# Loading a head's tiles half a head ahead, parking three outputs in DRAM, and moving softmax arithmetic from VectorE to ScalarE and GpSimd, in the attention stage of a hybrid transformer layer

## The chip, the cores and the metric

The kernel runs on one core of a Trainium2 chip. The core has a matrix engine (TensorE, PE in the profile, with its weight loads counted apart as PEld), VectorE (DVE), ScalarE (ACT), GpSimd (POOL) and SyncE (SP, which here only issues DMAs). Each engine works through its own queue in order, and semaphores tie the queues together. The metric is the device time of one launch in microseconds (us); less is better.

## The reference

One encoder layer on 1024 tokens of width 1024, in float32: a half-step SwiGLU feed-forward, a mixer, a second feed-forward, a final RMSNorm. The change is in the mixer, between its input projection and its output projections:

```python
# A: 8 heads of 64, each 64-token chunk sees itself and 8 chunks before it
p = softmax(q k^T / 8 + bias_A);            y_a = p v
# B: 4 heads, two score maps each, values of width 128, chunk-causal
p = softmax over keys of (q k^T / 8 + bias_B), for r = 0, 1
y_b = rms_norm((p[0] - lam * p[1]) v, subln_g) * (1 - lambda_init)
x = x + (sigmoid(g_A) * (y_a W_A) + sigmoid(g_B) * (y_b W_B)) W_o
```

## The kernel before

The work is in stages one after the other: feed-forward 1, mixer projection, attention, the two branch projections and W_o, feed-forward 2. Attention is the block that opens the PSUM pool `ps2` (line 750). The projection has left q, k, a second copy of k (low-order part) and v in DRAM; attention reads them per "head" of the loop, of which there are eight: four pairs of A heads (`jobs_a(pr)`) and four B heads (`jobs_b(hb, filler)`).

A job is a Python generator; each `yield` ends one of its steps. An A job (block pair `sb_`, head `h`) does scores, softmax and scaling for two blocks of 128 queries (lines 840 to 849), passes a step, transposes the probabilities (853 to 855), passes on, and multiplies by v (857 to 877). A B job (query block `i`, with `(i + 1) * 128` keys) does two scores and two softmaxes (914 to 920), two reciprocals (922, 924), the factor r2 = -lam * rs0 / rs1 (925) and the sum pr[0] += r2 * pr[1] (927) in one VectorE instruction; then, a step later, transposes (933), then the product with v (940 to 944), the scaling by r1 and the norm (945 to 955), and last a small matmul `try` that transposes and scales the output into y (957 to 960).

`run` (811) interleaves the jobs: it starts one job per round and moves up to four older ones a step on, the newest first. This gives the program order. A list scheduler then puts every engine's queue in order by a simulated timeline, with program order as priority: an instruction goes into the queue when its inputs, and a free buffer for what it writes, are there in that simulation.

Buffers that matter: `big` (line 70) has 14 slots of 8 KB per partition. A head holds four of them (qs, ks, kl, vt, loaded by `load_qkv`, 757), one for its bias rows nb (A: one per pair; B: one per two heads; `bias_rows`, 798, eight DMAs and some memsets on GpSimd), and one for its output y. All eight outputs stay in slots until the branch projections. The loads of a head are issued by its own first job (823 to 829, 901 to 909), so they are queued behind the jobs before, as far as priority goes, and need free slots.

`branch_a` (881) is the filler: the product of the A outputs with W_A, 16 pieces of 12 matmuls (lines 128 to 130 through `mm3`), handed out at half a piece per B job (934 to 937). It needs only the A outputs. The product with W_B follows when attention is done (975 on). `split` (94) writes a value as a rounded high part and a rest: ScalarE rounds (97 or 99), VectorE or GpSimd subtracts (102 or 104). `rsqrt` (137) is a GpSimd `pow` on a column of 128 values.

Of the kernel before, what the change touches and what calls it, by code (L numbers as in the profile page):

```python
# [9 lines left out]
F32 = mybir.dt.float32  # L10
F32R = mybir.dt.float32r
AF = mybir.ActivationFunctionType
ALU = mybir.AluOpType
# [41 lines left out]
def hybrid_layer_kernel(ctx, tc, x, ffn1_norm, ffn1_w_in, ffn1_w_out, mix_norm, w_mix_in,  # L55
# [35 lines left out]
    nc.vector.memset(neg_half, -0.5)  # L91

# [426 lines left out]
    def drams(n, shape, name, dtype=F32):  # L519
        return [dram.tile(shape, dtype, name=f"{name}{i}") for i in range(n)]  # L520
# [53 lines left out]
    ta_d = drams(KT, [P, S], "ta")  # L574
    diag_a = dram.tile([A_HEADS, SKEW, EA], F32, name="diag_a")
# [173 lines left out]
    ys = []  # L749
    with tc.tile_pool(name="ps2", bufs=1, space=PSUM) as ps:  # L750
# [60 lines left out]
        def run(jobs, filler=None):  # L811
            live = []
            for step, job in enumerate(list(jobs) + [None] * 4):
                for g in [job] + live[::-1] if job else live[::-1]:
                    next(g, None)
                live = (live + [job] if job else live)[-4:]


        def jobs_a(pr):
            ctx_ = {}  # L820

            def job(sb_, h):
                if not ctx_:
                    ctx_["qkv"] = load_qkv(pr)
                    ctx_["y"] = big([P, 2, S], "y")
                    ys.append(ctx_["y"])
                    ctx_["nb"] = big([P, 2, S], "nb", F32)
                    for hh in range(2):
                        bias_rows(ctx_["nb"][:, hh, :WA], diag_a, 2 * pr + hh, EA, WA)
# [9 lines left out]
                pms = []  # L839
                for s, i in enumerate((i0, i1)):  # L840
# [6 lines left out]
                    nc.vector.reciprocal(out=ri, in_=rs)  # L847
# [30 lines left out]
            return [job(sb_, h) for sb_ in range(4) for h in range(2)]  # L878
# [18 lines left out]
        def jobs_b(hb, filler):  # L897
            ctx_ = {}

            def job(i):  # L900
                if not ctx_:
                    ctx_["qkv"] = load_qkv(4 + hb)
                    ctx_["y"] = big([P, 2, S], "y")
                    ys.append(ctx_["y"])
                    if hb % 2 == 0:
                        nbs.append(big([P, 2, S], "nb", F32))
                        for hh in range(2):
                            bias_rows(nbs[-1][:, hh, :], diag_b, hb + hh, EB, WB)
                    ctx_["nb"] = nbs[-1][:, hb % 2, :]
# [3 lines left out]
                pr, rs = [], []  # L913
                for r in range(2):
                    sc, n = scores(qkv, r, i, 0, w)
                    pm = raw_tile([P, WB], "pm")[:, :w]
                    s_ = small.tile([P, 1], F32, tag="rs", name="rs")
                    softmax(sc, n, nb[:, WB - w:], pm, s_)
                    pr.append(pm)
                    rs.append(s_)  # L920
                r1, r2 = (small.tile([P, 1], F32, tag="ri", name="ri") for _ in range(2))
                nc.vector.reciprocal(out=r1, in_=rs[0])

                nc.vector.reciprocal(out=r2, in_=rs[1])  # L924
                nc.vector.scalar_tensor_tensor(out=r2, in0=r2, scalar=neg_lam, in1=rs[0],
                                               op0=ALU.mult, op1=ALU.mult)
                nc.vector.scalar_tensor_tensor(out=pr[0], in0=pr[1], scalar=r2, in1=pr[0],
                                               op0=ALU.mult, op1=ALU.add)
# [27 lines left out]
                yield  # L956
                tr = ps.tile([P, 4, P], F32, tag="pt", bufs=2, name="try")
# [3 lines left out]
            return [job(i) for i in range(NT)]  # L961

        jobs, nbs = [], []
        for pr in range(4):
            jobs += jobs_a(pr)
        filler = branch_a()
        due = [0]
        for hb in range(4):
            jobs += jobs_b(hb, filler)
        run(jobs)  # L970
        for _ in filler:
            pass

# [82 lines left out]
```

## Time and profile before

| quantity | us |
| --- | --- |
| three timed runs | 2149.18, 2153.07, 2155.61 |
| median | 2153.07 |
| profiled execution | 2152.95 |
| its span in the trace | 2151.1 |
| PE / DVE / ACT / POOL busy over the span | 2080.7 / 1442.3 / 980.2 / 181.4 |
| attention, from the first score matmul to the last write of y | 1075.8 to 1352.6 |
| of it, B heads' first softmax at | 1182.04, 1208.73, 1253.23, 1294.49 |

The profiled execution lies within 0.2 us of the median of the timed runs. A view of the trace by stretches of time gives, for each engine, the busy us in that stretch (how many instructions in brackets), the clock granted to TensorE as a share of full speed, the mean share of time in which the 16 DMA engines were busy, and GB/s. Views of groups give a line of the kernel, an engine, an operation, out<-in by the program's names, how many, the busy us and the mean ns of one, and the idle time in front of it with what ended it. A timeline row is start, duration, engine, line, operation. TensorE's busy time is modelled from pipelined matmuls and overstates its work; the weight loads (PEld) follow it more closely, since each matmul has one.

### The profile page before, as it was taken

Reading aid. Unit: us, or ns where it says so; the run is one execution under the profiler, and the core shown is the slowest. Engines: PE = TensorE matmul, PEld = TensorE weight load, DVE = VectorE, ACT = ScalarE, POOL = GpSimd, SP = SyncE. Lnnn points to the kernel's source line nnn. Section 1 sums busy time; section 2 is a strip of 40 time slices with the busy share of each in tenths; the row PEclk is TensorE's granted clock in tenths of the full one; section 3 lists DMA queues with packets and bytes.
Section 4 is the critical chain, followed back from the end, with each engine's and each line's share of the span. In section 5 each row is a group of like instructions: output and inputs, shape, how many; then the busy total and the mean of one; then the engine's idle time right before and its main releaser. Section 6 shows DMA issues by size and latency. Waiting matters only on the chain.

```text
span 2151.1 us, 29100 instructions
## 1 busy us (share of the span) xinstructions
PE 2080.7 (97%) x10073; PEld 1738.7 (81%) x10073; DVE 1442.3 (67%) x2650; ACT 980.2 (46%) x1919; POOL 181.4 (8%) x282
## 2 busy tenths in 40 slices
PE   6999999999999999999999988999999999999997
PEld 5788888888888788899788877788788888888886
DVE  7666566677577756566488977558766656658566
ACT  5433333334446544444498665146433333334444
POOL 2120000000001000000066233001000000000001
PEclk9999999999999999999999999999999999999999
DMA  6653333294445544553683364634543333366334
GB/s 194 173 169 111 95 96 120 93 327 143 117 128 162 168 142 164 198 196 136 230 275 105 136 211 133 233 119 151 172 156 95 111 96 95 114 237 228 98 117 158
DMA packets 277555, 333.55 MB, mean 155 GB/s; under 512 B 15404, under 2 KB 167996, under 8 KB 277408
## 3 DMA queue, kind: packets, MB, share of 16 engines
q1 hardware_dynamic: 276080, 327.94, 46.7%
q0 software_dynamic: 1184, 3.24, 0.6%
q8 instruction: 79, 1.29, 0.3%
q14 instruction: 68, 0.56, 0.1%
q10 hardware_dynamic: 144, 0.52, 0.1%
HBM read 226.45 MB, written 105.19 MB: 154 GB/s over the span
## 4 chain that ended last, share of the span: by engine, by line
PE 82%; DVE 6%; DMA 4%; ACT 3%; issue 2%; SPq 1%; POOL 0%; ACTq 0%; DVEq 0%; POOLq 0%
PE prod L128 18%; PE prod L129 18%; PE prod L130 18%; PE po L129 7%; PE po L128 7%; PE po L130 7%; DVE wlo L102 2%; PE pb L128 1%; PE pb L130 1%; PE pb L129 1%; ACT pm L789 1%; DMA raw<-in_ffn_w_in_dram 1%; ACT whi L97 1%; PE tr L205 1%; PE pt L795 1%
## 5 line engine op out<-in xcount | busy, mean ns | idle before, releaser
L129 PE MATMUL po<-wlo,whi 128*128 128x512 f32 x744 | 290.6, 391 | 2.2 <-DVE wlo L102 2.2
L130 PE MATMUL po<-whi,wlo 128*128 128x512 f32 x744 | 289.4, 389 | 0.0
L97 ACT CAST whi<-raw 128x512 fp32r<-128x512 f32 x200 | 124.3, 622 | 308.1 <-PE prod L129 238.3
L97 ACT CAST whi<-B 128x512 fp32r<-128x512 f32 x186 | 115.8, 623 | 272.0 <-PE po L129 265.4
L97 ACT CAST whi<-T 128x512 fp32r<-128x512 f32 x192 | 119.4, 622 | 244.2 <-PE prod L129 224.7
L102 DVE TENSOR_TENSOR wlo<-B,whi 128x512 fp32r<-128x512 f32 x186 | 128.0, 688 | 139.3 <-ACT whi L97 139.2
L113 DVE TENSOR_TENSOR c<-prod,c 128x512 f32<-128x512 f32 x190 | 131.1, 690 | 133.6 <-PE prod L130 121.1
L102 DVE TENSOR_TENSOR wlo<-raw,whi 128x512 fp32r<-128x512 f32 x200 | 137.0, 686 | 106.6 <-ACT whi L97 64.0
L128 PE MATMUL po<-whi 128*128 128x512 f32 x744 | 201.5, 390 | 0.0
L102 DVE TENSOR_TENSOR wlo<-T,whi 128x512 fp32r<-128x512 f32 x192 | 131.8, 687 | 92.1 <-ACT whi L97 90.8
L129 PEld LDWEIGHTS po<-wlo,whi 128*128 128x128 f32 x744 | 139.6, 188 | 33.7 <-DVE wlo L102 5.1
L139 POOL TENSOR_TENSOR r<-v,neg_half 128x1 f32<-128x1 f32 x64 | 49.7, 780 | 1383.0 <-DVE v L180 1264.7
L130 PEld LDWEIGHTS po<-whi,wlo 128*128 128x128 f32 x744 | 139.7, 188 | 28.7
L128 PEld LDWEIGHTS po<-whi 128*128 128x128 f32 x744 | 139.1, 188 | 28.8 <-ACT whi L97 0.2
L102 DVE TENSOR_TENSOR wlo<-N,whi 128x512 fp32r<-128x512 f32 x64 | 44.1, 689 | 113.6 <-PE prod L129 62.9
L102 DVE TENSOR_TENSOR wlo<-ha,whi 128x512 fp32r<-128x512 f32 x154 | 105.4, 684 | 9.0 <-ACT whi L97 9.0
L272 ACT COPY c<-prod 128x512 f32<-128x512 f32 x186 | 103.1, 586 | 11.2 <-DMA hA<-c 4.4
L97 ACT CAST whi<-ha 128x512 fp32r<-128x512 f32 x154 | 94.8, 615 | 16.9 <-PE prod L129 11.4
L789 ACT ACTIVATE pm<-pm,mn 128x640 f32<-128x640 f32 (+7 forms) x128 | 94.0, 736 | 11.8 <-DVE ri L924 6.1
L128 PE MATMUL prod<-S1h,whi 128*128 128x512 f32 x240 | 94.4, 393 | 2.4 <-ACT S1h L97 1.4
L787 DVE CUSTOM_DVE_ANT_0 pm<-sc,nb 128x640 f32<-128x640 f32 (+7 forms) x128 | 87.9, 698 | 11.4 <-PE sc L780 8.8
L128 PE MATMUL prod<-S2h,whi 128*128 128x512 f32 x240 | 94.0, 392 | 1.3 <-ACT whi L97 1.3
(237 smaller groups left out, 5338.9 us busy)
## 6 DMA issues: line engine op xcount, KB each, us to landing
raw<-in_ffn_w_in_dram SPq DMA_DIRECT2D x98, 512.0 KB, 4.3
raw<-in_w_mix_in_dram SPq DMA_DIRECT2D x47, 512.0 KB, 4.4
ha<-hS SPq DMA_DIRECT2D x88, 256.0 KB, 2.6
hA<-c SPq DMA_DIRECT2D x66, 256.0 KB, 4.2
ha<-hA SPq DMA_DIRECT2D x66, 256.0 KB, 2.7
B<-in_ffn_w_out_dram SPq DMA_DIRECT2D x12, 1024.0 KB, 10.2
hS<-hs SPq DMA_DIRECT2D x44, 256.0 KB, 2.7
hS<-c SPq DMA_DIRECT2D x44, 256.0 KB, 4.4
```

The costliest lines, as they stand in the source:

```text
L97: nc.scalar.copy(out=hi, in_=src)
L102: (nc.gpsimd if on_pool else nc.vector).tensor_tensor(out=lo, in0=src, in1=h, op=ALU.subtract)
L113: nc.vector.tensor_tensor(out=out_, in0=a, in1=b, op=op)
L128: nc.tensor.matmul(ps, a[0], b[0], start=first, stop=False, skip_group_check=shared)
L129: nc.tensor.matmul(ps, a[0], b[1], start=False, stop=False, skip_group_check=shared)
L130: nc.tensor.matmul(ps, a[1], b[0], start=False, stop=last, skip_group_check=shared)
L139: nc.gpsimd.tensor_tensor(out=r, in0=v, in1=neg_half, op=ALU.pow)
L205: nc.tensor.transpose(tr[:, k, :], rows[:, k * P:(k + 1) * P], ident)
L272: nc.scalar.copy(out=self.held[name], in_=p)
L787: nc.vector.tensor_tensor_reduce(out=d3, in0=sc, in1=nb.rearrange("p (n w) -> p n w", n=n), scale=1.0, scalar=3e38, op0=ALU.add, op1=ALU.m ...
L789: nc.scalar.activation(out=dst, in_=dst, func=AF.Exp, bias=mn, scale=-1.0, accum_out=rs)
L795: nc.tensor.transpose(pt[:, b, :], p, ident)
```

## The change

1. Loads. What a head needs loaded moves out of its first job into a function `begin`, and the list of jobs puts a head's `begin` after the fourth of the eight jobs of the head before. Head 0's loads are cut in two halves each.
2. Outputs of B heads 0 to 2 are stored to DRAM (`y_d`) when their last block is written, and their slots are given back. They are loaded again in the middle of the last head. Only the last head's y stays.
3. B softmax: one GpSimd `pow` with exponent -1 on two columns takes the place of the two VectorE reciprocals; the fused VectorE line 927 becomes a ScalarE copy with scale r2 on pr[1] and a GpSimd addition into pr[0].
4. B jobs get one more empty step ahead of `try`; `run` keeps five older jobs moving and not four.
5. A softmax: both row sums go into one tile and one VectorE reciprocal inverts both; the two GpSimd scalings come after it.

```diff
@@
+    y_d = drams(3, [P, 2, S], "y", F32R)
...
+        def run(jobs):
             live = []
-            for step, job in enumerate(list(jobs) + [None] * 4):
+            for job in list(jobs) + [None] * 5:
+                if callable(job):
+                    job()
+                    continue
                 for g in [job] + live[::-1] if job else live[::-1]:
                     next(g, None)
-                live = (live + [job] if job else live)[-4:]
+                live = (live + [job] if job else live)[-5:]
...
+            def begin():
+                ctx_["qkv"] = load_qkv(pr, 1 if pr else 2)
+                ctx_["nb"] = big([P, 2, S], "nb", F32)
+                for hh in range(2):
+                    bias_rows(ctx_["nb"][:, hh, :WA], diag_a, 2 * pr + hh, EA, WA)
...
-                    rs = small.tile([P, 1], F32, tag="rs", name="rs")
-                    softmax(sc, n, nb[:, h, WA - w:WA], pm, rs)
-                    ri = small.tile([P, 1], F32, tag="ri", name="ri")
-                    nc.vector.reciprocal(out=ri, in_=rs)
-                    nc.gpsimd.tensor_tensor(out=pm, in0=pm, in1=ri.to_broadcast([P, w]), op=ALU.mult)
+                    softmax(sc, n, nb[:, h, WA - w:WA], pm, rs[:, s:s + 1])
                     pms.append(pm)
+                ri = small.tile([P, 2], F32, tag="ri", name="ri")
+                nc.vector.reciprocal(out=ri, in_=rs)
+                for s, pm in enumerate(pms):
+                    nc.gpsimd.tensor_tensor(out=pm, in0=pm, in1=ri[:, s:s + 1].to_broadcast(list(pm.shape)), op=ALU.mult)
...
+            def begin():
+                ctx_["qkv"] = load_qkv(4 + hb)
+                if hb % 2 == 0:
+                    nbs.append(big([P, 2, S], "nb", F32))
+                    for hh in range(2):
+                        bias_rows(nbs[-1][:, hh, :], diag_b, hb + hh, EB, WB)
+                ctx_["nb"] = nbs[-1][:, hb % 2, :]
...
-                nc.vector.reciprocal(out=r1, in_=rs[0])
-                nc.vector.reciprocal(out=r2, in_=rs[1])
-                nc.vector.scalar_tensor_tensor(out=r2, in0=r2, scalar=neg_lam, in1=rs[0],
+                ri = small.tile([P, 2], F32, tag="rj", bufs=6, name="ri")
+                nc.gpsimd.tensor_tensor(out=ri, in0=rs, in1=neg_one, op=ALU.pow)
+                r1, r2 = ri[:, 0:1], small.tile([P, 1], F32, tag="r2", name="r2")
+                nc.vector.scalar_tensor_tensor(out=r2, in0=ri[:, 1:2], scalar=neg_lam, in1=rs[:, 0:1],
                                                op0=ALU.mult, op1=ALU.mult)
-                nc.vector.scalar_tensor_tensor(out=pr[0], in0=pr[1], scalar=r2, in1=pr[0],
-                                               op0=ALU.mult, op1=ALU.add)
+                nc.scalar.activation(out=pr[1], in_=pr[1], func=AF.Copy, scale=r2)
+                nc.gpsimd.tensor_tensor(out=pr[0], in0=pr[0], in1=pr[1], op=ALU.add)
...
                 yield
+                yield
                 tr = ps.tile([P, 4, P], F32, tag="pt", bufs=2, name="try")
...
+                if i == NT - 1 and hb < 3:
+                    move(nc.sync, y_d[hb], y)
...
+        def load_y(hb):
+            ys.append(big([P, 2, S], "y"))
+            move(nc.sync, ys[-1], y_d[hb])
...
+        jobs = [heads[0][0]]
+        for n, (_, js) in enumerate(heads):
+            jobs += js[:4] + ([heads[n + 1][0]] if n < 7 else []) + js[4:6]
+            jobs += [lambda hb=hb: load_y(hb) for hb in range(3) if n == 7] + js[6:]
         run(jobs)
```

More of the change, by code (lines that the diff above doesn't have):

```diff
@@ L91, in hybrid_layer_kernel @@
     nc.vector.memset(neg_half, -0.5)
+    neg_one = const.tile([P, 2], F32, name="neg_one")
+    nc.vector.memset(neg_one, -1.0)
     def split(src, hi, lo, scale=None, on_pool=False):
@@ L807, in bias_rows @@
                                               [[length - 1, SKEW], [1, c1 - c0]]))
-        def run(jobs, filler=None):
+        def run(jobs):
             live = []
-            for step, job in enumerate(list(jobs) + [None] * 4):
+            for job in list(jobs) + [None] * 5:
+                if callable(job):
+                    job()
+                    continue
                 for g in [job] + live[::-1] if job else live[::-1]:
                     next(g, None)
-                live = (live + [job] if job else live)[-4:]
+                live = (live + [job] if job else live)[-5:]
         def jobs_a(pr):
             ctx_ = {}
+            def begin():
[3 more added lines that the diff above has]
+                    bias_rows(ctx_["nb"][:, hh, :WA], diag_a, 2 * pr + hh, EA, WA)
             def job(sb_, h):
-                if not ctx_:
-                    ctx_["qkv"] = load_qkv(pr)
+                if "y" not in ctx_:
                     ctx_["y"] = big([P, 2, S], "y")
                     ys.append(ctx_["y"])
-                    ctx_["nb"] = big([P, 2, S], "nb", F32)
-                    for hh in range(2):
-                        bias_rows(ctx_["nb"][:, hh, :WA], diag_a, 2 * pr + hh, EA, WA)
                 qkv, y, nb = (ctx_[n] for n in ("qkv", "y", "nb"))
@@ L877, in job @@
                     split(ysum, y[:, 0, c], y[:, 1, c], on_pool=True)
-            return [job(sb_, h) for sb_ in range(4) for h in range(2)]
+            return begin, [job(sb_, h) for sb_ in range(4) for h in range(2)]
         def branch_a():
@@ L898, in jobs_b @@
             ctx_ = {}
+            def begin():
[5 more added lines that the diff above has]
+                ctx_["nb"] = nbs[-1][:, hb % 2, :]
             def job(i):
-                if not ctx_:
-                    ctx_["qkv"] = load_qkv(4 + hb)
+                if "y" not in ctx_:
                     ctx_["y"] = big([P, 2, S], "y")
[L904 to L909, printed above, removed]
+                    if hb == 3:
+                        last_y.append(ctx_["y"])
                 qkv, y, nb = (ctx_[n] for n in ("qkv", "y", "nb"))
@@ L912, in job @@
                 w = (i + 1) * P
-                pr, rs = [], []
+                pr = []
+                rs = small.tile([P, 2], F32, tag="rs", name="rs")
                 for r in range(2):
@@ L960, in job @@
                 split(tr[:, 0, :], y[:, 0, c], y[:, 1, c], scale=gsub)
[L961 to L965, printed above, removed]
+                if i == NT - 1 and hb < 3:
+                    move(nc.sync, y_d[hb], y)
+            return begin, [job(i) for i in range(NT)]
+        def load_y(hb):
+            ys.append(big([P, 2, S], "y"))
+            move(nc.sync, ys[-1], y_d[hb])
+        nbs = []
         filler = branch_a()
         due = [0]
-        for hb in range(4):
-            jobs += jobs_b(hb, filler)
+        heads = [jobs_a(pr) for pr in range(4)] + [jobs_b(hb, filler) for hb in range(4)]
+        jobs = [heads[0][0]]
+        for n, (_, js) in enumerate(heads):
+            jobs += js[:4] + ([heads[n + 1][0]] if n < 7 else []) + js[4:6]
+            jobs += [lambda hb=hb: load_y(hb) for hb in range(3) if n == 7] + js[6:]
         run(jobs)
```

9 lines of the change are left out of this document (4 added, 5 removed).

## The prediction

> **What bounds the kernel now.** I began with the page's slices of the span, 53.8 us each:
>
> ```profile
> PE   6999999999999999999999988999999999999997
> ```
>
> Apart from the ends, TensorE falls below nine tenths in two slices, from 1237 to 1344 us, in the B heads. So I cut that stage into stretches, at the first and the last softmax of each B head. First row: one A head, for comparison. Then B head 0; head 1, from its first to its last softmax; the gap to head 2; head 2; the gap to head 3; head 3; the tail.
>
> ```profile
> core 0: us, PE busy (x) PEld busy (x) DVE busy (x) ACT busy (x) POOL busy (x), PEclk, DMA share, GB/s
> 1077.90:1104.43 26.53, 24.97 (x180) 22.09 (x181) 23.56 (x77) 23.77 (x65) 18.99 (x25) 1.00 0.94 332
> 1182.00:1208.70 26.70, 24.55 (x138) 20.73 (x138) 24.58 (x79) 19.60 (x54) 6.47 (x11) 1.00 0.52 189
> 1208.70:1238.40 29.70, 28.47 (x180) 25.39 (x179) 27.05 (x87) 17.52 (x53) 9.29 (x17) 1.00 0.29 92
> 1238.40:1253.20 14.80, 10.18 (x62) 8.12 (x61) 9.64 (x29) 9.49 (x25) 6.52 (x12) 1.00 1.02 326
> 1253.20:1282.80 29.60, 28.55 (x169) 25.88 (x169) 25.77 (x84) 18.57 (x52) 9.13 (x17) 0.94 0.32 104
> 1282.80:1294.50 11.70, 9.97 (x49) 7.91 (x49) 7.34 (x25) 7.08 (x17) 3.47 (x6) 0.85 1.02 377
> 1294.50:1323.50 29.00, 28.02 (x172) 24.39 (x171) 25.84 (x85) 18.34 (x54) 10.33 (x19) 1.00 0.23 81
> 1323.50:1353.00 29.50, 20.52 (x124) 17.47 (x124) 17.18 (x47) 14.31 (x38) 10.38 (x19) 0.94 0.58 190
> ```
>
> Inside a head TensorE is 96% busy and VectorE 87 to 91%. In the two gaps both fall away while the DMA share is 1.02. The timeline of VectorE has the last softmax before each gap and the first one behind it:
>
> ```profile
> 1237.18 1.22 DVE L787 CUSTOM_DVE_ANT_0 pm<-sc,nb 128x1024 f32<-128x1024 f32 x1
> 1253.23 0.29 DVE L787 CUSTOM_DVE_ANT_0 pm<-sc,nb 128x128 f32<-128x128 f32 x1 [1.99 <-DMA nb<-diag_b]
> ...
> 1281.59 1.22 DVE L787 CUSTOM_DVE_ANT_0 pm<-sc,nb 128x1024 f32<-128x1024 f32 x1
> 1294.49 0.29 DVE L787 CUSTOM_DVE_ANT_0 pm<-sc,nb 128x128 f32<-128x128 f32 x1 [0.78 <-PE sc L780]
> ```
>
> No softmax starts for 16.1 and 12.9 us. The chain of waits over this stretch shows why, and the DMA queue's timeline shows that the loads are issued only at the end of the head before:
>
> ```profile
> 1197.15 11.17 DMA kl<-kx
> ...
> 1238.61 4.89 SPq L805
> ...
> 1244.01 9.06 DMA nb<-diag_b
> ```
>
> ```profile
> 1234.61 0.43 SPq L124 DMA_DIRECT2D qs<-q  x1
> ...
> 1237.47 14.33 SPq L805 DMA_DIRECT2D nb<-diag_b  x8
> ...
> 1280.59 0.42 SPq L124 DMA_DIRECT2D qs<-q  x1
> ```
>
> That is a slot matter: at head 2 the 14 slots hold four A outputs, two or three B outputs, bias rows and four tiles of head 1, so head 2's tiles wait for head 1's scores to end. The gaps aren't lost whole, since TensorE has fillers. I measure the loss by weight loads. The three stretches inside heads load 25.39 + 25.88 + 24.39 = 75.66 us in 88.3 us, a rate of 0.857. At that rate the gaps' 8.12 and 7.91 us need 9.5 and 9.2 us, so 5.3 and 2.5 us are lost (about 3 in the second, whose loads ran at clock 0.85). Head 0 loses 26.7 - 20.73 / 0.857 = 2.5, the tail 29.5 - 20.4 = 9.1. All of B, 129.9 us of weight loads, would take 151.6 us at that rate; it takes 171.0.
>
> **The change part by part.** The prices, from the groups of the B stage (1182 to 1353):
>
> ```profile
> L927 DVE SCALAR_TENSOR_TENSOR pm<-pm,ri 128x128 f32<-128x128 f32 (+7 forms) x32 | 26.6, 832 | 0.3
> L139 POOL TENSOR_TENSOR r<-v,neg_half 128x1 f32<-128x1 f32 x32 | 23.6, 737 | 40.6 <-DVE v L952 34.3 <-DVE ri L924 4.0 <-PE try L958 1.5
> L949 POOL TENSOR_TENSOR o<-o,o 128x128 f32<-128x128 f32 x32 | 14.7, 460 | 62.6 <-ACT o L948 62.6
> L946 ACT ACTIVATE o<-pv,ri 128x128 f32<-128x128 f32 x32 | 11.8, 368 | 4.9 <-PE pv L944 4.9
> L922 DVE RECIPROCAL ri<-rs 128x1 f32<-128x1 f32 x32 | 5.0, 157 | 0.3
> L924 DVE RECIPROCAL ri<-rs 128x1 f32<-128x1 f32 x32 | 5.0, 156 | 6.3 <-ACT o L948 6.1
> L102 POOL TENSOR_TENSOR y<-ysum,y 128x256 fp32r<-128x256 f32 x1 | 0.7, 741 | 8.7 <-ACT y L97 8.7
> ```
>
> and from those of the whole span:
>
> ```profile
> L197 ACT ACTIVATE xc<-xc,r 128x512 f32<-128x512 f32 x12 | 8.1, 713 | 0.3 <-POOL r L139 0.3
> ...
> L847 DVE RECIPROCAL ri<-rs 128x1 f32<-128x1 f32 x64 | 9.9, 155 | 1.4 <-ACT pm L789 1.0
> ```
>
> *Loads half a head ahead.* Heads 1 and 3 of B find four free slots at that point (four A outputs, one B output still being stored or one being written, bias rows, the running head's four tiles: 10 of 14), so their 4 MB start some 15 us sooner and land inside the head before, where the DMA share is 0.23 to 0.32. Taken off: 5.3 and 3 us for the gaps and 1 of head 0's 2.5 (its end waits on kl, but its VectorE is also 92% busy): **-9.3**, between -6 and -10.8. In A nothing goes: the same load of a head is there long before its first softmax. The y traffic adds three stores and three loads of 1 MB, about 3.2 us each at the gap's 326 GB/s, beside a mostly idle DMA; they cost nothing unless SP stands at a store with loads queued behind, up to 2 us.
>
> *What is late next.* Head 2 wants a fifth slot, for new bias rows, and head 1's y wants one as well; 10 + 4 + 2 is 16. One comes free with head 0's stored y, the other only when head 1's last scores are done. If the bias rows lose, their eight DMAs (9.06 us in the chain, with q, k and v alongside) stand alone in the old gap: 5 to 9 us without softmax, of which the gap's ratio 5.3 / 14.8 is lost, 1.8 to 3.2 us. If y loses, the `try` results of two jobs sit in the two PSUM buffers that transposes use, for about two jobs: up to 5 us. **+2.5**, 0 to +5.
>
> *A's reciprocals.* Eight fewer VectorE instructions a head, 1.24 us of 155 ns each. ScalarE, at 23.77 of 26.53 us, is as full as VectorE and loses nothing, so I take a third: **-1.5** over four heads, 0 to -5. The first GpSimd scaling waits for the second softmax; the transposes come two rounds (6.6 us) later, which covers it.
>
> *B's softmax arithmetic.* VectorE loses (26.6 + 5.0 + 5.0) / 4 = 9.15 us a head. ScalarE gains eight copies: from 368 ns at 128 and 713 at 512, 0.9 ns an element over a fixed 0.25, so 6.2 us for widths of 128 to 1024. GpSimd gains eight two-input additions: 460 ns at 128 and 741 at 256 make 0.28 us for each block of 128 columns over a fixed 0.18; the 36 blocks and 8 instructions of a head are 11.5 us. And eight two-column `pow`: no such width is in the trace; between one column's 0.74 and twice it, 5.9 to 11.8 us, and I take 5.9, since other GpSimd work shows most of a narrow instruction to be fixed. Adding to a mean head (sums of the rows over four):
>
> | a B head, us | before | after |
> | --- | --- | --- |
> | VectorE | 34.3 | 25.2 |
> | ScalarE | 26.2 | 32.4 |
> | GpSimd | 13.9 | 31.3 (to 37.2) |
>
> against 37.9 us, a quarter of 151.6. The A row shows that this program can run ScalarE at 0.90. So nothing but TensorE binds, yet VectorE's relief is worth little, because TensorE idles only 3.3 of the 88.3 us inside heads: at most 6 of 151.6 us. **-2**, 0 to -6. The empty round ahead of `try` is part of this: it gives GpSimd time for the norm behind longer additions.
>
> *The tail.* The last job trades 1.28 us (line 927 at 1024) and two reciprocals for a `pow` 0.74, a copy 1.17 and an addition 2.4: 2.7 us more in a chain with little beside it. **+1.5**, -2 to +3.
>
> Sum: -9.3 + 2.5 - 1.5 - 2 + 1.5 = -8.8, and with the smaller costs rounded down, -9. The profiled execution took 2152.95, the median is 2153.07, so one number serves for both: **2144**. All best ends give -23.8, all worst about +4: 2129 to 2157.
>
> [...] Two pairs of rows from the timelines:
>
> ```profile
> 1296.94 1.28 DVE L927 SCALAR_TENSOR_TENSOR pm<-pm,ri 128x1024 f32<-128x1024 f32 x1
> 1297.10 1.53 POOL L139 TENSOR_TENSOR r<-v,neg_half 128x1 f32<-128x1 f32 x1 [1.33 <-DVE v L952]
> ...
> 1324.26 0.48 DVE L925 SCALAR_TENSOR_TENSOR ri<-ri,neg_lam,rs 128x1 f32<-128x1 f32 x1
> 1324.27 0.45 POOL L949 TENSOR_TENSOR o<-o,o 128x128 f32<-128x128 f32 x1 [0.29 <-ACT o L948]
> ```
>
> The `pow` that began under line 927 ended 0.41 us behind it, at twice its mean; the one-column line 925 ended just when the addition on GpSimd did. [...]
>
> **The rivals.** *VectorE locked out (0.18).* [...] At w = 0.8 B takes 183 us: +10, **2163**.
>
> *The loads were hidden anyway, or wait on (0.20).* The fillers did much of the gaps' work; if head 2's tiles or bias rows still come late for want of slots, only head 1's and 3's 4 us go: -4 + 2.5 - 1.5 - 2 + 1.5 = -3.5, **2149**. For: 16 wants on 14 slots. Against: q, k and v were most of the gap's bytes.
>
> *The forecast (0.62)*: the gaps close and nothing new binds.
>
> A difference of 0.3%, 6.5 us, is about what can be told from none. So faster 0.62, same 0.20, slower 0.18. The range reaches from the best end, 2129, to the first rival's 2163, leaving out only w above 0.8.
>
> **What would show it.** Right: B's first softmaxes 34 to 38 us apart with no stretch over 5 us without one; qs loads of a B head some 15 us before its first score; TensorE busy above 95% from 1182 until the tail; B, from its first softmax to the last y, near 163 us. Slot cost: a pause ahead of head 2 alone, ended by nb. Wrong: lines 925 and 952 at means over 0.8 us; GpSimd above 90% with TensorE or VectorE waiting on it; or a B stage at 171 us or more with the loads early.

## The result, and the profile after

Ahead of the change 2152.71 us (median of 6 runs, 2149.18 to 2155.61), after it 2161.76 (6 runs, 2159.29 to 2164.02): ratio 1.004, 95% interval 1.0029 to 1.005, so 6 to 11 us slower. The forecast was 2144.0, faster. That the measured time lies inside the range of 2129 to 2163, near its upper end, is luck: the cause is another one, as will be seen. The profiled execution of the kernel after has a span of 2159.3 us, 8.2 more than the one before.

The page's 40 slices, read alone, say that the change did its work: TensorE is now below nine tenths in one inner slice and not in two.

```profile
PE   6999999999999999999999989999999999999997
```

In VectorE's timeline of the kernel after, the last softmax of B heads 1 and 2 and the first of heads 2 and 3:

```profile
1239.02 1.23 DVE L790 CUSTOM_DVE_ANT_0 pm<-sc,nb 128x1024 f32<-128x1024 f32 x1 [0.17 <-PE sc L783]
1245.96 0.29 DVE L790 CUSTOM_DVE_ANT_0 pm<-sc,nb 128x128 f32<-128x128 f32 x1 [0.66 <-DMA nb<-diag_b]
...
1279.54 1.22 DVE L790 CUSTOM_DVE_ANT_0 pm<-sc,nb 128x1024 f32<-128x1024 f32 x1
1282.23 0.29 DVE L790 CUSTOM_DVE_ANT_0 pm<-sc,nb 128x128 f32<-128x128 f32 x1
```

The gaps of 16.1 and 12.9 us have become 6.9 and 2.7, and what is left ahead of head 2 ends with nb, as forecast. But the time didn't fall. The view by stretches, with the columns of the prediction, has the A heads, B up to the last softmax, and the tail; first before, then after:

```profile
1077.00:1190.00 113.00, 105.62 (x751) 93.86 (x751) 100.02 (x320) 99.22 (x263) 74.17 (x93) 1.00 0.54 182
1190.00:1322.00 132.00, 120.55 (x712) 104.80 (x712) 111.36 (x349) 84.33 (x228) 44.01 (x80) 0.97 0.48 164
1322.00:1364.00 42.00, 32.83 (x178) 27.31 (x177) 22.65 (x57) 16.77 (x41) 11.59 (x21) 0.92 0.53 173
```

```profile
1077.00:1190.00 113.00, 105.35 (x725) 91.02 (x726) 97.03 (x283) 101.39 (x266) 77.87 (x96) 1.00 0.67 224
1190.00:1322.00 132.00, 121.72 (x711) 104.33 (x709) 93.25 (x260) 100.50 (x251) 87.97 (x124) 0.96 0.42 148
1322.00:1364.00 42.00, 33.20 (x174) 27.37 (x175) 19.64 (x51) 18.91 (x47) 21.37 (x34) 0.89 0.74 269
```

VectorE is 18 us lighter in the second stretch, as was meant, and TensorE loads as many weights in the same 132 us as before (104.33 to 104.80). In the A stage, where nothing was to change, it loads 2.84 us of weights less in the same time, and the first A output of each head follows the one of the head before after 27.9 us and not 26.5 (heads 2 and 3).

**Where the time goes** is seen best by lining the kernels up by work. I took all score matmuls, products with v and branch products from the first score matmul on, weighed each by the median duration of its kind in the kernel before, and read off the time at which a given share of them is done. The table gives how far each kernel is behind the one before (us, mean over the band of shares). Before reaches the middles of the bands 138, 189, 225, 251 and 298 us after its first score matmul: behind A, behind the first old gap, behind the second, in the tail, and in the branch product behind attention. The lags and the last column, which is dealt with below, come from one profiled execution of each kernel; the timed runs of one kernel differ by several us, so a lag of 2 or 3 us is little, and the order of the work moves single values by about 1 us. Each ratio is to the runs of before that were timed together with that kernel. Two slow executions, one of e1 and one of e7, are left out of the medians.

| kernel | median, ratio to before [95%] | 40-46% | 54-62% | 66-72% | 76-80% | 84-96% | lost to half clock |
| --- | --- | --- | --- | --- | --- | --- | --- |
| before | 2152.7 | 0 | 0 | 0 | 0 | 0 | 6.8 |
| after | 2161.8, 1.0040 [1.0029, 1.0050] | 5.2 | 2.9 | 3.1 | 7.7 | 6.8 | 10.2 |
| e1_merge_only | 2159.1, 1.0027 [1.0016, 1.0039] | 4.5 | 3.7 | 5.5 | 8.0 | 6.2 | 11.9 |
| e2_loads_only | 2156.7, 1.0023 [1.0014, 1.0033] | 2.9 | 0.1 | -0.1 | 4.9 | 2.5 | 8.5 |
| e3_arith_only | 2166.4, 1.0063 [1.0048, 1.0078] | 1.9 | 8.6 | 10.0 | 14.3 | 13.8 | 20.5 |
| e4_no_merge | 2161.0, 1.0045 [1.0029, 1.0061] | 3.5 | 3.2 | 3.4 | 7.3 | 6.6 | 8.5 |
| e5_no_arith | 2160.3, 1.0032 [1.0021, 1.0044] | 2.9 | 2.4 | 2.3 | 6.4 | 7.0 | 6.8 |
| e6_no_yield | 2177.5, 1.0112 [1.0096, 1.0128] | 5.9 | 10.1 | 14.2 | 23.6 | 23.2 | 20.5 |
| e7_a_late | 2164.3, 1.0049 [1.0031, 1.0067] | 3.6 | 6.4 | 6.6 | 13.4 | 11.9 | 13.6 |
| e8_strict | 2154.7, 1.0011 [1.0001, 1.0020] | 5.9 | 4.1 | 2.8 | 1.4 | 0.6 | 5.1 |
| e9_drain_a | 2160.4, 1.0037 [1.0023, 1.0050] | 5.9 | 3.5 | 3.7 | 7.6 | 6.9 | 6.8 |
| e10_before_strict | 2161.6, 1.0037 [1.0022, 1.0052] | 9.1 | 8.3 | 7.5 | 7.7 | 8.0 | 17.1 |
| e11_all_late | 2167.6, 1.0066 [1.0051, 1.0081] | 7.9 | 8.0 | 9.4 | 9.6 | 12.9 | 15.4 |
| e12_drain_strict | 2170.0, 1.0073 [1.0056, 1.0090] | 20.4 | 18.3 | 19.4 | 19.1 | 17.1 | 13.7 |
| e13_b_early | 2158.4, 1.0021 [1.0011, 1.0030] | 0.6 | 0.9 | 0.4 | 7.4 | 5.7 | 10.2 |
| e14_b_early_strict | 2153.1, 0.9999 [0.9990, 1.0008] | 3.0 | 0.4 | -1.0 | -2.5 | -0.6 | 5.1 |
| e15_b_early_strict_old | 2153.5, 1.0003 [0.9994, 1.0012] | 0.8 | 0.0 | 0.3 | 1.0 | 1.1 | 13.7 |
| e16_dummy | 2157.0, 1.0016 [1.0007, 1.0026] | 2.6 | 1.8 | 0.8 | 0.8 | -0.2 | 6.8 |
| e17_a_early | 2162.1, 1.0038 [1.0025, 1.0051] | 5.5 | 4.8 | 7.6 | 8.3 | 9.5 | 13.7 |
| e18_before_strict_b | 2157.4, 1.0014 [1.0005, 1.0023] | 4.5 | 4.0 | 3.5 | 3.7 | 3.8 | 15.4 |

The row of after is the result in short: 5 us are lost by the end of A, the closed gaps give back 2 (where 8.3 were forecast, and 2.5 of cost for the slots), and the tail loses 5 more.

**What TensorE waits for** is told by the waits ahead of its weight loads (total us, times, longest). In the A stage, 1077 to 1190 us, before and after:

```profile
PEld sc L779 <- DVE mn L787: 2.1, 7, 0.5
```

```profile
PEld sc L782 <- DVE mn L790: 6.7, 24, 0.5
PEld pt L798 <- POOL pm L858: 4.5, 11, 0.5
PEld pt L798 <- DVE wlo L104: 3.2, 8, 0.5
```

Scores stand at the head of TensorE's queue until a softmax on VectorE gives back one of the two PSUM buffers for scores: 24 times and not 7. All listed waits of this stage add up to 14.9 us before and 19.6 after. From 1190 to 1322 us they are 16.8 and 17.1, so closing the gaps took away no waiting. Before, in the first gap itself (1238.4 to 1253.2), they are these:

```profile
PEld try L958 <- POOL dg L955: 2.4, 2, 1.6
PEld pv L943 <- ACT o L948: 1.1, 2, 0.7
PEld pt L795 <- DVE wlo L102: 0.6, 2, 0.3
PEld pb L128 <- ACT o L948: 0.5, 1, 0.5
```

These are the ends of the older jobs' chains, 4.6 us in all. Only the wait that follows them is one for the loads, at one remove: 1.73 us that end at 1253.58, just past this window, at scores that want a PSUM buffer. The softmax that frees it started at 1253.23, after 1.99 us of waiting for nb. With the slow piece of the clock behind it, shown below, this wait is worth 3.4 us. After, from 1190 to 1364 us, the list has others in their place:

```profile
PEld sc L782 <- DVE mn L790: 5.9, 13, 1.1
PEld try L970 <- POOL dg L966: 3.4, 3, 1.6
PEld pb L130 <- DVE gl L901: 3.1, 2, 2.9
PEld pv L954 <- ACT o L959: 2.7, 7, 0.6
PEld pb L130 <- ACT o L959: 2.3, 4, 0.8
```

**The clock.** The third of these is one stall. SP's timeline of the kernel after shows its origin:

```profile
1200.28 0.37 SPq L126 DMA_DIRECT2D qs<-q  x1
...
1237.35 0.37 SPq L126 DMA_DIRECT2D vt<-v  x1
1237.77 0.57 SPq L121 DMA_DIRECT2D gl<-g  x1
1238.78 5.40 SPq L808 DMA_DIRECT2D nb<-diag_b  x8
```

Head 2's qs goes out 34 us ahead of the old 1234.61, but its vt only when a slot is free, at 1237.35; the filler's gate values gl and the bias rows stand behind it on SP. TensorE then stands at the filler, whose PSUM buffer VectorE frees only when gl has landed (timelines of VectorE and TensorE, after):

```profile
1243.88 0.69 DVE L901 TENSOR_TENSOR gl<-pb,gl 128x512 f32<-128x512 f32 x1 [1.96 <-DMA gl<-g]
1244.63 0.50 PE L130 MATMUL pb<-y,whi 128*128 128x512 f32 x1 [2.76 <-DVE gl L901]
```

What follows is in the granted clock, the third column from the end, of the stretches around it:

```profile
1241.50:1245.00 3.50, 0.74 (x6) 0.55 (x5) 1.34 (x4) 3.01 (x8) 3.42 (x6) 1.00 1.08 289
1245.00:1248.50 3.50, 3.50 (x10) 2.77 (x9) 2.20 (x8) 1.43 (x5) 3.12 (x3) 0.52 0.84 245
```

The same in the kernel before, behind a wait of 1.73 us:

```profile
1253.58 0.38 PE L779 MATMUL sc<-ks,qs 128*128 128x256 f32 x1 [1.73 <-DVE mn L787]
```

```profile
1251.00:1254.50 3.50, 1.77 (x13) 1.51 (x13) 1.47 (x9) 1.51 (x7) 0.45 (x1) 1.00 0.71 167
1254.50:1258.00 3.50, 3.50 (x17) 3.50 (x17) 2.86 (x11) 2.30 (x7) 1.69 (x2) 0.52 0.75 262
```

Half speed comes in pieces of about 3.4 us, each worth 1.7 us of TensorE. Stretches of 0.5 us from 1060 to 1420 us show four such pieces before (6.8 us) and six after (10.2): the last column of the table. Before, the wait of 1.73 us has such a piece behind it, and the 1.4 us of idle time that end at 1245.64 have none. What tells the two apart in these traces is how much of the 3.41 us ahead TensorE is busy. The slow pieces start at whole multiples of 3.41 us from one another: before, at 1254.61, 1285.33, 1336.53 and 1353.59 us, which is 9, 15 and 5 times 3.413 us apart. So the time can be divided into stretches of that length; these are the ones with either wait, in the kernel before:

```profile
1244.38:1247.79 3.41, 1.89 (x8) 1.46 (x9) 2.49 (x10) 2.38 (x7) 1.89 (x4) 1.00 1.07 360
1251.21:1254.62 3.41, 1.68 (x12) 1.42 (x12) 1.38 (x10) 1.63 (x7) 0.45 (x1) 1.00 0.69 167
```

The first, 55% busy, keeps the clock, and the second, 49% busy, loses it. In the 20 traces there are 1779 such stretches at full speed between 1065 and 1400 us. All 65 with TensorE busy below 0.515 are followed by a slow piece, 28 of the 124 between that and 0.72, and none of the 1590 above.

### The profile page after: what moved, and what is told of

Its sections match the earlier page's. It is cut to its first block, busy times and chain, and to the rows that moved or that the text cites. A ratio compares the mean times of both kernels' runs of the same rounds, so it can differ in the third digit from the quotient of the medians.

```text
span 2159.3 us, 29120 instructions
## 1 busy us (share of the span) xinstructions
PE 2089.9 (97%) x10073; PEld 1741.3 (81%) x10073; DVE 1422.2 (66%) x2523; ACT 1001.6 (46%) x1951; POOL 238.9 (11%) x346
## 4 chain that ended last, share of the span: by engine, by line
PE 85%; DVE 7%; issue 2%; ACT 2%; DMA 2%; POOL 1%; SPq 0%; ACTq 0%; DVEq 0%; POOLq 0%
PE prod L130 18%; PE prod L131 18%; PE prod L132 18%; PE po L131 6%; PE po L130 6%; PE po L132 6%; DVE wlo L104 2%; PE pb L130 2%; PE pt L798 1%; PE pb L131 1%; PE sc L782 1%; PE pb L132 1%; PE sc L783 1%; PE tr L207 1%; PE pv L954 1%
## 5 line engine op out<-in xcount | busy, mean ns | idle before, releaser
L141 POOL TENSOR_TENSOR r<-v,neg_half 128x1 f32<-128x1 f32 x64 | 44.3, 695 | 1358.1 <-DVE v L182 1266.3
L792 ACT ACTIVATE pm<-pm,mn 128x640 f32<-128x640 f32 (+7 forms) x128 | 94.1, 737 | 10.1 <-DVE mn L790 9.3
```

The source lines that it names most:

```text
L141: nc.gpsimd.tensor_tensor(out=r, in0=v, in1=neg_half, op=ALU.pow)
L792: nc.scalar.activation(out=dst, in_=dst, func=AF.Exp, bias=mn, scale=-1.0, accum_out=rs)
```

## The experiments

Letters in the expectations: M, the merged reciprocals lengthen A; B, longer chains in B; L, early loads with their slots and SP queue; R or O, the order in which queues are filled; D, the early transfers themselves; C, half-clock pieces; H, the gaps were not lost work; S, strictness helps only with early loads. Results are in the table above. In the code, three dots stand for lines left out.

### One edit alone

e1_merge_only is the kernel before with edit 5 alone:

```diff
...
-                    nc.vector.reciprocal(out=ri, in_=rs)
-                    nc.gpsimd.tensor_tensor(out=pm, in0=pm, in1=ri.to_broadcast([P, w]), op=ALU.mult)
...
+                nc.vector.reciprocal(out=ri, in_=rs)
+                for s, pm in enumerate(pms):
+                    nc.gpsimd.tensor_tensor(out=pm, in0=pm, in1=ri[:, s:s + 1].to_broadcast(list(pm.shape)), op=ALU.mult)
```

> The kernel before with one edit of the change, A's merged reciprocal. Theory M (the merged reciprocal lengthens A: one VectorE instruction behind two softmaxes, both GpSimd scalings behind it): an A head takes 27.9 us and not 26.5, the time is 2157 to 2160, against some 2153 of the kernel before. Theory B (the loss is in the B stage, by longer chains over ScalarE and GpSimd) and theory L (by the early loads and their slots): A head at 26.5 or a little less, time 2149 to 2153.

It is slower by 0.27%, as theory M said, but the A heads take 25.6, 29.0 and 26.9 us, 27.2 on average and not 27.9. Its waits in the A stage have these at the top (1.9 and 2.8 us in the kernel before):

```profile
PEld pt L795 <- DVE wlo L102: 4.2, 11, 0.8
PEld pt L795 <- POOL pm L850: 4.2, 9, 0.8
```

Transposes do wait longer, for the later scalings on GpSimd (second line) and for VectorE to free their PSUM buffers (first line). Three more slow pieces of the clock come on top.

e2_loads_only is edits 1 and 2 alone: early `begin`, outputs through DRAM, VectorE's arithmetic, four older jobs, no merge.

```diff
...
+            jobs += js[:4] + ([heads[n + 1][0]] if n < 7 else []) + js[4:6]
+            jobs += [lambda hb=hb: load_y(hb) for hb in range(3) if n == 7] + js[6:]
```

> The kernel before with the loads half a head ahead and three y through DRAM; softmax arithmetic of A and B, and the number of empty steps, as before. If the loads do what was forecast of them: gaps ahead of B heads 2 and 3 close, 2143 to 2148. Theory L (early loads fill the 14 slots, the loads of vt and bias rows stand on SP for a slot and the fillers' loads behind them, and the order of A changes too): 2152 to 2160. Theories M and B expect the former.

The step that was to bring -9.3 us costs 0.23%, a time in theory L's range. A heads 2 and 3 take 27.8 us each; the gaps close (3 us between softmaxes); the row of the table shows 2.9 lost in A, the same regained in B, and 5 lost in the tail, of which half come back.

e3_arith_only is edit 3 alone:

```diff
...
-                nc.vector.scalar_tensor_tensor(out=pr[0], in0=pr[1], scalar=r2, in1=pr[0],
-                                               op0=ALU.mult, op1=ALU.add)
+                nc.scalar.activation(out=pr[1], in_=pr[1], func=AF.Copy, scale=r2)
+                nc.gpsimd.tensor_tensor(out=pr[0], in0=pr[0], in1=pr[1], op=ALU.add)
```

> The kernel before with B's softmax arithmetic moved to ScalarE and GpSimd, nothing else. Theory B: B's stretches between first and last softmax get longer (29.5 us a head before, then 32 or more), 2156 to 2165. Theories M and L: the relief of VectorE is worth its 0 to 6 us, 2147 to 2153.

Slower by 0.63%, the dearest of the three and a little above theory B's range. Twelve slow pieces of the clock lose 20.5 us, 13.7 more than before, of the 15.5 by which its span is longer. Its SP timeline shows where a second cost sits:

```profile
1240.83 0.32 SPq L895 DMA_DIRECT2D ta<-gl  x1
1248.56 0.38 SPq L121 DMA_DIRECT2D wa<-in_w_branch_a_dram  x1
1249.00 0.50 SPq L126 DMA_DIRECT2D qs<-q  x1
```

The filler's next weights stand ahead of head 2's loads and go out only at 1248.56, and head 2's first softmax comes at 1269.49 and not 1253.23.

### One edit undone

e4_no_merge: after without edit 5. e5_no_arith: after without edit 3. e6_no_yield: after without edit 4, whose removal is this:

```diff
-            for job in list(jobs) + [None] * 5:
+            for job in list(jobs) + [None] * 4:
...
-                live = (live + [job] if job else live)[-5:]
+                live = (live + [job] if job else live)[-4:]
...
                 yield
-                yield
                 tr = ps.tile([P, 4, P], F32, tag="pt", bufs=2, name="try")
```

> The changed kernel with A's merged reciprocal undone. Theory M: A head back from 27.9 to 26.5 us, 2153 to 2157 against 2161.8 of the changed kernel. Theories B and L: no more than 1 us off, 2160 to 2162.

> The changed kernel with B's softmax arithmetic back on VectorE; loads, y through DRAM, merged reciprocal and the extra step stay. Theory B (with the loads early the moved arithmetic still costs, as it cost 14 us alone): 2150 to 2156 against 2161.8. Rival: alone it cost so much because the loads stood behind the fillers' loads on SP, which early loads avoid, so that here it is worth nothing or a gain: 2160 to 2168.

> The changed kernel without the extra empty step ahead of the last matmul of a B job, four older jobs kept moving and not five. If the step hides GpSimd's norm behind the additions as supposed, this is slower, 2163 to 2168. If it only holds back y and the slot it sits in, so that vt and bias rows of heads 2 and 3 come late, this is faster, 2155 to 2160. If the planner's order makes up for it either way: 2160 to 2163.

e4 and e5 are level with after within the intervals: in the full change neither the merge nor the arithmetic decides, and A heads 2 and 3 stay at 27.8 to 27.9 us in both. Theories M and B fall as the main cause. e6 is 0.72% slower than after, 9 us above the worst of its expectation. This is TensorE's longest wait from 1190 to 1322 us; it comes to 5.9 us in the kernel after:

```profile
PEld sc L782 <- DVE mn L790: 14.0, 18, 4.2
```

The extra step is the one edit that the rest needs. e6 and e2 tell for what: both have early loads and no extra step, and they differ by the moved arithmetic and the merge. They lie 0.89% apart, 19 us. With the step, each of the two is worth nothing (e4, e5).

e11_all_late: after with edit 1 alone undone.

```diff
-            jobs += js[:4] + ([heads[n + 1][0]] if n < 7 else []) + js[4:6]
+            if n:
+                jobs.append(heads[n][0])
+            jobs += js[:6]
```

> The kernel after with its first edit alone undone: every head's loads come directly ahead of the head itself; outputs through DRAM, the moved arithmetic, the extra step and the merged reciprocals stay. The prediction's term for the loads (-9.3 us): about 2170. Theory H (the gaps were not lost work: work that waits behind a gap runs faster afterwards, and the early loads save some 3 us in B and cost some 4 in A): 2158 to 2164, with the gaps in front of B heads 2 and 3 back at 12 us or more and the A heads near 27 us.

1.0066 against 1.0040: in this setting the early loads are worth 0.26%, 5.6 us. The time is near the 2170 of the forecast's term, but that isn't the old gaps alone. A's heads of 25.6, 29.0 and 26.9 us are those of e1, with the merge and late loads, and the gaps in B are 23 and 10 us. How the rest of its loss divides between the moved arithmetic and the gaps, no run separates.

### Why A is slower

e7_a_late: after, with only B heads 1 to 3 loaded early. e13_b_early: the same without edit 5.

```diff
+            if 0 < n < 5:
+                jobs.append(heads[n][0])
-            jobs += js[:4] + ([heads[n + 1][0]] if n < 7 else []) + js[4:6]
+            jobs += js[:4] + ([heads[n + 1][0]] if 3 < n < 7 else []) + js[4:6]
```

> The changed kernel with the loads of A heads 1 to 3 and of B head 0 put back directly ahead of their own head; B heads 1 to 3 stay half a head early. Theory R (early loads change the order that the planner writes in A, softmaxes of the next head run ahead of the products of this one, and that order is slower on the chip) and theory D (the early transfers themselves disturb A): an A head back from 27.9 to 26.5 us, 2155 to 2158. If A's longer heads are not from the loads: no change, 2160 to 2163.

> The kernel after with A as it was before: the loads of A heads 1 to 3 and of B head 0 directly ahead of their own head, and A's reciprocals not merged; B's early loads, outputs through DRAM, moved arithmetic and extra step stay. If A's slower heads are the cause of the loss: A heads back at 26.5 us, last A output at 1190, and a time of 2156 to 2158, 4 to 6 us below the kernel after. If what A loses only decides when B starts, and B takes as long from there (as in the earlier run in which A's loads came late and the reciprocals stayed merged, 2164.9): A heads back at 26.5 us and a time of 2161 to 2164 all the same.

In e13 A is back at 26.5 us a head and waits 2.0 us at scores; the time is 0.24% below e4 (3.6 us by the medians), which differs only in A's and B head 0's loads. So some 4 or 5 us of the loss are A's. e7, which keeps the merge, has e1's A heads (25.6, 29.0 and 26.9 us) and misses both of its forecasts: without early loads the merge costs more than it does with them. e13 shows a second thing: up to the band 66-72% it is level with before, though its gaps are closed (7.0 and 1.1 us between the softmaxes), and then it loses 7 us in the tail.

e17_a_early: before, with A heads 1 to 3 alone loaded early. e16_dummy: before, with as many bytes in the middle of A heads 0 to 2, into slots that nothing reads.

```diff
+        def dummy(pr):
+            for src in (q_d[pr + 1], k_d[pr + 1], kx_d[pr + 1], q_d[pr]):
+                move(nc.sync, big([P, 2, S], "dm"), bass.AP(src.tensor, src.offset, [[S, P], [P * S, 2], [1, S]]))
...
+            jobs += ja[:4] + ([lambda pr=pr: dummy(pr)] if pr < 3 else []) + ja[4:]
```

> The kernel before, with the loads of A heads 1 to 3 alone half a head early; all else as before, B's loads too. Theory O and theory D alike: A heads 2 and 3 at 27.8 us; in this run TensorE's waits at scores for VectorE between 1077 and 1190 us rise from 2.1 us in the kernel before to 5 or 6 by theory O, and stay near 2 by theory D. Time 2155 to 2157 if the 1.3 us a head stay lost, 2152 to 2154 if B gets them back.

> The kernel before, with four more transfers of 1 MB in the middle of each of A heads 0 to 2, from the same tensors that the next head loads, into spare slots that nothing reads; the real loads stay where they were, so A's DMA bytes nearly double. Theory D (transfers in the middle of a head slow it down): A heads 1 to 3 at 27.9 us and 2156 to 2158. Theory O (the order of the queues does it): A heads at 26.5 us and a time within 2 us of the kernel before.

e16's A stage has a DMA share of 0.82, above the 0.67 of after:

```profile
1077.00:1190.00 113.00, 104.30 (x740) 93.72 (x740) 97.81 (x309) 96.58 (x254) 74.09 (x93) 0.98 0.82 290
```

and its heads 2 and 3 take 26.51 us, so theory D falls, although the time lies in its range of 2156 to 2158. A cause for the 0.16% shows in the first head, which is 2.7 us longer than before: the real ks is issued on SP behind the extra transfers, at 1080.53 and not at 1076.63, and TensorE waits for it, with a slow piece of the clock right behind.

```profile
1096.11 0.76 PE L779 MATMUL sc<-ks,qs 128*128 128x128 f32 x2 [1.52 <-DMA ks<-k]
```

This profile is the quickest of e16's ten executions, so its last bands end level. e17, with fewer bytes, has heads 2 and 3 of 27.75 and 29.07 us, and in its A stage

```profile
PEld sc L779 <- DVE mn L787: 4.8, 16, 0.5
```

close to the 5 or 6 us of the order theory. It costs 0.38%, as much as the whole change and more than was expected, though B's loads are as late as before: A's 5 us, and 4 more as B's loads come later (waits for ks and kl of 6.3 us).

e9_drain_a: after, with two empty rounds ahead of A heads 1 to 3 and of B head 0.

```diff
+            jobs += [None] * (2 if 0 < n < 5 else 0)
```

> The kernel after, with two empty rounds ahead of A heads 1 to 3 and of B head 0, so that a head's last jobs are through before the next head's first scores come up, while its loads still come half a head ahead. Theory O (with the loads early the scheduler mixes the next head's scores into the end of the running one, and that costs an A head 1.4 us): the A heads go back from 27.9 to about 26.5 us, and the time falls by 3 to 6 us, to 2156 to 2159. Theory D (the early transfers themselves slow an A head down): the A heads stay at 27.9 us or grow by the empty rounds, and the time is 2162 to 2168.

A stays at 28.1 us and the time at that of after. By its expectation that speaks for D, which e16 excludes. A reading that fits both is that empty rounds in program order don't bind the scheduler, which queues scores as soon as loads and buffers allow; the trace has 4.4 us of waits at scores and other waits in place of the rest, and no more than that is shown.

### The order on TensorE

e8_strict: after, with a job's scores queued behind the last product with v of the round before. e10_before_strict: the same on before. e12_drain_strict: e8 and e9 together. In e14, e15 and e18 the rule holds in B alone.

```diff
+            if last_pv:
+                with tc.issue_after(last_pv[-1].ins):
+                    return scores_(qkv, h, i, k0, w)
...
+                last_pv.append(mm)
```

> The changed kernel with TensorE's order held to the program's rounds: the scores of a job are queued behind the last product with v of the round before (an order on TensorE's queue alone, no wait added). The loads stay early. Theory R: A heads come back to some 26.5 to 27 us, because the run-ahead is gone, and 2153 to 2158. Theory D: A heads stay at 27.9. Rival to R: any stricter order starves VectorE and both get longer, 2165 or more.

> The kernel before, with the order on TensorE alone made strict: a job's scores are queued behind the last product with v of the round before, as in the earlier run that did this to the kernel after (2154.7). Theory C (what the order changes are the half-clock windows and the gaps that make them, so a stricter order helps any of these kernels): 2146 to 2150, with fewer half-clock windows than the four of the kernel before. Theory S (strictness helps only where the early loads have mixed the heads): the kernel before hardly changes, 2151 to 2155.

> The kernel after with both: two empty rounds ahead of A heads 1 to 3 and B head 0, and the strict order of scores on TensorE. If the A heads' 1.4 us each and the half-clock windows are two separate costs (theory O beside theory C): 2149 to 2152, below the kernel before. If they are the same cost, or the empty rounds only move the loss to another place: 2154 to 2158.

e8 takes 7 us off after; A is no better (27.8 us a head, though its waits at scores are down to 1.6 us), but B regains 5 and the tail loses nothing. On before the same rule costs 0.37%. Theory C falls; theory S is nearer, but its 2151 to 2155 is missed by 7 us, since strictness also costs A time there (first bands 9.1). e12 misses both of its forecasts and is 0.73% slower than before: strictness and empty rounds together lengthen A's heads to 30.4, 31.7 and 29.3 us. So strictness gained only in B, and only with early loads. That a strict queue can't run ahead to fill a wait for loads is the likely reason, and isn't tested.

> The run with only B's loads early, and in addition the strict order of scores on TensorE in B alone (a job's scores behind the last product with v of the round before). If TensorE standing at scores whose PSUM buffer VectorE still holds is what B loses, and strictness cures it there: 2145 to 2149, below the kernel before. If strictness gained on the kernel after only by chance of order and clock windows: 2155 to 2163.

> The run with B's loads early and strict scores in B, with B's softmax arithmetic back on VectorE (reciprocals and fused line as before; the extra step stays). The prediction's term for the arithmetic (-2 us): 2154 to 2157. If VectorE, some 9 us a head fuller, is what then holds scores back: 2158 or more. If the moved arithmetic is worth nothing or costs by its longer chain: 2150 to 2153, below the kernel before.

> The kernel before with the strict order of scores on TensorE in B alone; loads late, arithmetic and A as before. If the order alone made the earlier run with B early and strict as good as it was, and the early loads add nothing: 2151 to 2155. If strictness only works with the loads early (a strict queue stops TensorE's run ahead into the gap while it waits for loads): 2157 to 2163, and the early loads are worth the difference to 2153.1.

e14 is e13 with strict scores in B: 0.9999, level with before and between its two forecasts, with no wait at scores among the longest between 1190 and 1364, which are now

```profile
PEld pv L961 <- ACT whi L99: 5.6, 8, 1.7
PEld pb L130 <- ACT o L967: 3.7, 5, 2.0
PEld try L978 <- POOL dg L974: 2.6, 2, 2.4
```

e18, the same rule on before, is 0.14% slower than before, as its second case said, so early loads in B, with the edits that go with them, are then worth 3 us. e15, with the arithmetic back on VectorE, is level with e14, against the 2154 to 2157 of the prediction's term: the arithmetic is worth nothing there either. No version here beats before.

## Why the prediction was wrong

**The loads, -9.3: the step that failed.** The prediction priced the gaps by weight loads "at that rate" of 0.857, as if TensorE could keep inside-head speed all through B once softmaxes came without a gap. The gaps did close. But of TensorE's waits in the first gap only 1.7 us hung on the loads, 3.4 with the slow piece behind them, and 4.6 us were the ends of job chains; from 1190 to 1322 us it waits as long after (17.1) as before (16.8), now at scores for VectorE and at the filler's gl. By the lag table the closed gaps give 2 us in after, 3 in e2, 4 in e14 and none in e13. The pause ahead of head 2 doesn't hide a larger gain: e2 and e14 have none there (3.0 and 2.8 us between the softmaxes). The rival "the loads were hidden anyway" had this right ("the fillers did much of the gaps' work"); it kept 4 us of gain and has to lose most of those as well. Alone, the edit costs 0.23%.

**"In A nothing goes": wrong by 5 us.** It looked at the transfers, which are indeed early enough, and not at what early data allow: with the next head's tiles there, its scores go into TensorE's queue ahead of older jobs' transposes and products. B's first softmax comes at 1174 us, 30 ahead of the last A output; before, it came at 1182, 8 ahead. The queue then stands at scores until VectorE has freed their buffer. e13, e17 and e16 show that the early loads cost A its time, and by the order, not by the transfers. That the waits at scores are the whole reason is not shown: in e8 they are down to 1.6 us, and other waits come instead (23.1 us in all, against 19.6). Why the A stage before has just the better mixture stays open.

**The slots, +2.5: right in place and within its range.** The pause ahead of head 2 alone is there, 6.9 us, ended by nb. But TensorE loses by another wait than the one forecast. What was missed is who else stands behind vt on SP: the filler's gl, with 2.8 us of idle TensorE and a slow piece of clock, 4.5 us together. No run took this away by itself. Nor did head 3 find four free slots, as was counted: its vt goes out at 1278.96, only 3 us ahead of the old 1282.16, though no pause came of it.

**A's reciprocals, -1.5: wrong sign alone** (e1, +0.27%), and unresolved within the change (e4 against after). "The transposes come two rounds later, which covers it" was too much: waits for the scalings rose from 2.8 to 4.2 us.

**The arithmetic, -2: prices right, value nil.** Two groups from 1182 to 1353 us, before, and five from 1190 to 1360, after:

```profile
L952 DVE CUSTOM_DVE_ANT_0 sq<-o 128x128 f32<-128x128 f32 x32 | 9.2, 286 | 0.0
L925 DVE SCALAR_TENSOR_TENSOR ri<-ri,neg_lam,rs 128x1 f32<-128x1 f32 x32 | 7.6, 236 | 0.3
```

```profile
L939 POOL TENSOR_TENSOR pm<-pm 128x512 f32<-128x512 f32 (+7 forms) x29 | 44.0, 1516 | 14.6 <-ACT pm L938 14.2 <-PE pt L798 0.3
L938 ACT ACTIVATE pm<-pm,r 128x512 f32<-128x512 f32 (+7 forms) x29 | 23.3, 804 | 3.2 <-DVE r L936 3.2
L933 POOL TENSOR_TENSOR ri<-rs,neg_one 128x2 f32<-128x2 f32 x28 | 19.7, 702 | 0.6 <-ACT pm L792 0.6
L963 DVE CUSTOM_DVE_ANT_0 sq<-o 128x128 f32<-128x128 f32 x32 | 14.3, 446 | 6.6 <-POOL o L960 6.5
L936 DVE SCALAR_TENSOR_TENSOR r<-ri,neg_lam,rs 128x1 f32<-128x1 f32 x29 | 6.8, 233 | 2.7 <-POOL ri L933 2.5
```

The two-column `pow` takes 702 ns (0.74 was taken), the additions 1.5 us. The 2163 of the first rival rests on w, a wait of lines 925 and 952 behind GpSimd's additions, put at 0.8 us; no run shows this wait. The rival's sign is absent: line 936 (925 before) has its old mean, 233 ns against 236, and line 963 (952 before) rose from 286 to 446 ns, 5 us over 32, far from a mean over 0.8 us. With the extra step the edit is worth 0 (e5, e15). Without it, it costs 13.6 us with late loads (e3) and, with the merge, 19 us with early ones (e6 against e2), which no rival had. In e3 most of the loss is clock; that a longer chain per job drains TensorE at each head's end is the likely way, and is argued.

**The tail, +1.5: too small.** From the start of the last softmax to the end of the last write of y it takes 38.2 us and not 30.7, and the lag rises by 4.6. It isn't the arithmetic (e5 loses 4.1), and it is gone where scores are strict and loads early (e8, e14). That scores taken early leave the last rounds little to fill waits with is argued, not shown.

**What was to show it.** B's first softmaxes are 27, 45 and 36 us apart, not 34 to 38; its stage, from the first softmax to the last y, takes 186 us, not 163, part of it beside A's end, which is 14 us later. So the prediction's own sign of failure came true, "a B stage at 171 us or more with the loads early"; GpSimd, at 67% between 1190 and 1322, was not the bound.

**Not in the sum: the clock.** The half-clock pieces came to between 5.1 and 20.5 us over these kernels. The table has one execution of each, but every timed run has a mean granted clock: 0.9939 on average in the 86 runs of before that were timed with the experiments, 0.9913 in the six of after. That is 13.2 and 18.7 us of full speed lost over the whole launch, 5.5 us apart, out of the 9 that after is slower. Not all of it is lost time: e15 loses 17.6 us by its timed runs and is level with before. That a slow piece costs nothing where TensorE would wait anyway is the likely reason, and isn't shown. Among the runs of one kernel (215 in all) the time rises by about 0.57 us for each us of clock lost. By that, an estimate, the clock is some 3 us of the 9. In e5 it is next to nothing (14.5 us lost, 1.3 more than before) and the time is up all the same, so the clock alone isn't the cause.

**Together.** The closed gaps with the slots were to give 6.8 us and gave 2, A lost 5 that were put at nothing, and the tail lost 3 more than forecast. The arithmetic and A's reciprocals, 3.5 us of forecast gain, came to nothing. That makes some 16 us, about the 17 between the forecast and the profiled execution.

## What to carry to other kernels

A stretch without work on one engine isn't lost time of the bound engine: list what the bound engine waits for inside the stretch, and count as gain only the waits that the change removes. Where a list scheduler fills in-order queues, earlier data change the order as well; ask which instruction will then stand at the head of the queue and for whose buffer. Test an edit in the company it will have: here the arithmetic cost 13.6 us without the extra step and nothing with it.

## What the runs showed of the hardware

TensorE's clock fell to half for about 3.4 us, with 1.7 us lost each time, behind stretches of that length whose longest idle time was, in the kernels before and after, only 0.9 to 2.8 us (after, 0.98 us at 1281.6 and 2.76 at 1241.9). Over the 20 traces, every one of the 65 such stretches with TensorE busy below 0.515 had a slow piece behind it, and none of the 1590 above 0.72. A DMA share of 0.82 over the whole A stage didn't lengthen A heads 2 and 3 (26.51 us at 0.82 as at 0.54). A `pow` on two columns took GpSimd 702 ns in the kernel after; one column took 737 before and 582 after (means over the B stage).
